# Scaling attention probabilities on ScalarE instead of VectorE and GpSimd

## The chip, the cores and the metric

One core of a Trainium2 chip runs the whole program. The metric is the device time of one execution in microseconds (us). The engines are TensorE (PE in the profile), VectorE (DVE), ScalarE (ACT), GpSimd (POOL) and SyncE (SP), which issues the DMAs. Each engine works through its own queue in order and waits for others by semaphores.

## The reference

Two layers of a hybrid backbone over 256 latent tokens and 256 context tokens of width 1024. Each layer has four parallel token mixers (differential attention, Hyena long convolution, a Conformer convolution, multi-head latent attention), a gated merge, an output projection, and a mixture of 16 experts. Layer 1 computes the latent tokens' outputs only. The change concerns two of the mixers:

```python
def attn_probs(q, k, scale):
    s = jnp.einsum('...qd,...kd->...qk', q, k).astype(jnp.float32) * scale
    return jax.nn.softmax(s, axis=-1)

def softmax_attend(q, k, v, scale):              # latent attention, 4 heads
    p = attn_probs(q, k, scale)
    return jnp.einsum('bhqk,bhkv->bhqv', p.astype(v.dtype), v)

def diff_attend(q, k, v, lam):                   # differential attention, 4 heads, two maps each
    p = attn_probs(q, k, DIFF_HEAD_DIM ** -0.5)
    a = p[:, :, 0] - lam * p[:, :, 1]
    return jnp.einsum('bhqk,bhkv->bhqv', a.astype(v.dtype), v)
```

Context queries see the 256 context keys only; latent queries see all 512 keys.

## The kernel before

Everything is float32; the large projections split each operand into a high and a low half and use three matmuls per product (`mm3`, L355 to L357). The halves are made by `split` (L346): ScalarE casts the high half (L348), VectorE subtracts for the low one (L349).

The program is written as generators, one for each thread of work: the input projection (`head`, `body`), `hyena`, `mla` (latent attention), `rope`, `diff` (differential attention), the four branch projections, the conformer, the modulation products (`products`, whose VectorE work is L510), and the experts with their router. A planner (`Order.run`, L175) keeps an estimated clock for each of PE, ACT, DVE and POOL. A generator emits some instructions and yields their estimated costs, as a dictionary by engine; the planner adds them to its clocks one after the other and picks as next the first generator in its list whose time has come. The order in which instructions are emitted is the order in each engine's queue, so the yielded costs fix the order of the whole program. The cost functions are `_a` for ScalarE, `_d` for VectorE and `_q` for GpSimd.

Attention is cut into units of 128 query rows and one head: 16 units in layer 0 (8 with 256 keys, 8 with 512), 8 in layer 1 (512 keys). Both loops are software pipelines over the units. In iteration i they scale the probabilities of unit i-1, transpose those of unit i-2 on TensorE (`transposed`, L1267: four transposes by matmul, then a ScalarE copy out of PSUM, L1272), multiply those of unit i-3 with the values, and compute scores and exponentials of unit i (`probs`, L1257: VectorE takes the row maximum, L1260, and negates it, L1262; ScalarE takes the exponential with a row sum, L1264).

In `mla` the scaling is a reciprocal of the row sum on VectorE (L1390) and a multiply of the probabilities by it (L1391). The multiply runs on VectorE in layer 0 and on GpSimd in layer 1, by the constant `MS = (0, 1)`.

In `diff` a unit has two maps, e0 and e1, and a pair of row sums. VectorE takes the reciprocals (L1493), multiplies e1 by its reciprocal and by minus lambda (L1494; `lamt` holds minus lambda), and adds e0 times its reciprocal to that (L1495). When the four heads of a query block are done, a head norm follows (L1531 to L1537), and its transposed outputs are split by L1509 on ScalarE and L1510 on VectorE.

Of the kernel before, what the change touches and what calls it, by code (L numbers as in the profile page):

```python
# [13 lines left out]
AF = mybir.ActivationFunctionType  # L14
OP = mybir.AluOpType
# [198 lines left out]
def _a(n):  # L214
    return 0.19 + n / 1200


def _d(n):
    return 0.07 + n / 960


def _q(n):
    return 0.1 + n / 480
# [3 lines left out]
def kernel(ctx: ExitStack, tc: tile.TileContext, x, ctxt, cols, skip, lamb, fng, ta, tb, tcn, td,  # L227
                       fwt, cc, ada_w, ada_t, w_in, w_uq, w_ukv, w_branch, w_out, w_ei, w_eo, out):
    nc = tc.nc
# [9 lines left out]
    LAG = (2.0, 1.0)  # L239
    PIECE = (4, 2)  # L240
    ORD = (0, 2)
    BA, MS, MVP = (1, 1), (0, 1), (1, 5)
    RINGS = ((1, 4), (2, 4))
    TGS, LOOK = (4, 10), 20.0
    GATE, F1, EXTRA, EARLY, EXTRA2 = 40, 9, (8, 8), (2, 3), (3, 4)
# [77 lines left out]
    lamt = const.tile([128, DEPTH], F32, name="lamt")  # L323
# [73 lines left out]
    def layer(l):  # L397
# [908 lines left out]
        def mla():  # L1306
# [17 lines left out]
            e = yield {"pe": 0.5, "dve": _d(512)}  # L1324
# [12 lines left out]
            e = yield rope_m(krT[R3, 256:])  # L1337
            km = [t2("km") for _ in range(4)]
            for hd in range(4):
# [4 lines left out]
                e = yield {"pe": 0.86, "act": _a(512), "pool": 0.8}  # L1344
# [40 lines left out]
            for i in range(n + 3):  # L1385
                end = []
                if 0 <= i - 1 < n:
                    nk = units[i - 1][2]
                    e, r = es.pop(i - 1)
                    nc.vector.reciprocal(r, r)  # L1390
                    (nc.gpsimd if MS[l] else nc.vector).tensor_scalar(e, e, r, None, op0=OP.mult)  # L1391
                    ws[i - 1], e = e, None
                    end.append((yield {"dve": 0.1, "pool" if MS[l] else "dve ": _q(nk) if MS[l] else _d(nk)}))
                if 0 <= i - 2 < n:
                    eTs[i - 2], cost = transposed(ws.pop(i - 2), units[i - 2][2])
                    end.append((yield cost))
                if 0 <= i - 3 < n and units[i - 3][3] % 2:
                    s, qc, nk, hd = units[i - 3]
                    oc, c = slice(qc - q0, qc - q0 + 128), hd // 2
                    if hd == 1:  # L1400
                        po = px()
                    pv = po[:, c * 128:(c + 1) * 128]
                    for k in range(nk // 128):
                        for j in range(2):
                            vo = (k % 2) * 256 + (2 * c + j) * 64
                            nc.tensor.matmul(pv[j * 64:(j + 1) * 64, :], mvt[k // 2][:, vo:vo + 64],
                                             eTs[i - 4 + j][:, k * 128:(k + 1) * 128],
                                             start=k == 0, stop=k == nk // 128 - 1, tile_position=(0, j * 64))
                    eTs.clear() if i - 2 >= n else [eTs.pop(u) for u in (i - 4, i - 3)]
                    hi, lo = o_ml[c]  # L1410
                    nc.scalar.copy(hi[:, oc], pv)
                    nc.vector.tensor_tensor(lo[:, oc], pv, hi[:, oc].bitcast(F32), op=OP.subtract)
                    end.append((yield {"pe": nk / 128 * 0.22, "act": _a(128), "dve": _d(128)}))
                if i < n:
                    s, qc, nk, hd = units[i]
                    p, r = psc(), sm(1, "re")
                    nc.tensor.matmul(p[:, :nk], qm[hd][:96, qc - q0:qc - q0 + 128], km[hd][:96, :nk], start=True, stop=True)
                    e, cost = probs(p, nk, scale, r)
                    es[i], p, e = (e, r), None, None
                    end.append((yield {"pe": nk * 0.00168, **cost}))  # L1420
                yield max(end) + LAG[l]
# [56 lines left out]
        def diff():  # L1478
            yield rope_ev["k"]
            yield rope_ev["q"]  # L1480
            rope_tab.clear()
            scale = 64.0 ** -0.5
            for c in range(4):
                o_df[c] = two("o")
            units = [(s, qc, nk, hd) for s, qc, nk in qblocks() for hd in range(4)]
            n = len(units)
            es, ws, eTs, os = {}, {}, {}, None
            for i in range(n + 4):
                end = []
                if 0 <= i - 1 < n:  # L1490
                    nk = units[i - 1][2]
                    e0, e1, r = es.pop(i - 1)
                    nc.vector.reciprocal(r, r)  # L1493
                    nc.vector.tensor_scalar(e1, e1, r[:, 1:2], lamt[:, l:l + 1], op0=OP.mult, op1=OP.mult)  # L1494
                    nc.vector.scalar_tensor_tensor(e0, e0, r[:, 0:1], e1, op0=OP.mult, op1=OP.add)  # L1495
                    ws[i - 1], e0, e1 = e0, None, None
                    end.append((yield {"dve": 0.1 + _d(nk) * 1.6}))
                if 0 <= i - 2 < n:
                    eTs[i - 2], cost = transposed(ws.pop(i - 2), units[i - 2][2])
                    end.append((yield cost))  # L1500
                if os is not None:
                    oc = slice(units[i - 4][1] - q0, units[i - 4][1] - q0 + 128)
                    p = pt()
                    for hh in range(4):
                        nc.tensor.transpose(p[:, hh * 128:(hh + 1) * 128], os[:, hh * 128:(hh + 1) * 128], ident)
                    for hh in range(4):
                        pv = p[:, hh * 128:(hh + 1) * 128]
                        hi, lo = o_df[hh]
                        nc.scalar.activation(hi[:, oc], pv, AF.Copy, scale=gsub)  # L1509
                        nc.vector.scalar_tensor_tensor(lo[:, oc], pv, gsub, hi[:, oc].bitcast(F32),  # L1510
                                                       op0=OP.mult, op1=OP.subtract)
                    os = None
                    end.append((yield {"pe": 0.5, "act": 4 * _a(128), "dve": 4 * _d(128)}))
                if i == 3:
                    for b in range(2):
                        yield dv_ev[b][0]
                    yield ml_done
                if 0 <= i - 3 < n:
                    s, qc, nk, hd = units[i - 3]
                    aT = eTs.pop(i - 3)  # L1520
                    if hd == 0:
                        po = px()
                    for k in range(nk // 128):
                        nc.tensor.matmul(po[:, hd * 128:(hd + 1) * 128], aT[:, k * 128:(k + 1) * 128],
                                         vd[k][:, hd * 128:(hd + 1) * 128], start=k == 0, stop=k == nk // 128 - 1)
                    aT = None
                    end.append((yield {"pe": nk / 128 * 0.21}))
                    if hd == 3:
                        os = t2("do")
                        ov = os.rearrange("p (h c) -> p h c", h=4)  # L1530
                        nc.scalar.activation(os, po, AF.Square)  # L1531
                        ss = sm(4, "ssd")
                        nc.vector.tensor_reduce(ss, ov, axis=AX.X, op=OP.add)
                        r = sm(4, "rsd")
                        rsqrt(r, ss, 1.0 / 128)
                        nc.vector.tensor_tensor(ov, po.rearrange("p (h c) -> p h c", h=4),
                                                r[:, :, None].to_broadcast([128, 4, 128]), op=OP.mult)  # L1537
                        end.append((yield {"act": _a(512), "dve": _d(512) + 0.1, "pool": 0.3, "dve ": _d(512)}))
                        if i - 3 == n - 1:
                            df_mid.t = S.t["pe"]  # L1540
                if i < n:
                    s, qc, nk, hd = units[i]
                    oc = slice(qc - q0, qc - q0 + 128)
                    pp, r = [psc(), psc()], sm(2, "re")
                    for c in range(2):
                        hs_ = slice(64 * c, 64 * c + 64)
                        nc.tensor.matmul(pp[c][:, :nk], qd[hd][hs_, oc], kd[hd][hs_, :nk], start=True, stop=True,
                                         tile_position=(64 * c, 0))
                    e0, cost = probs(pp[0], nk, scale, r[:, 0:1])
                    yield {"pe": nk * 0.00344, **cost}  # L1550
                    e1, cost = probs(pp[1], nk, scale, r[:, 1:2])
                    es[i], pp, e0, e1 = (e0, e1, r), None, None, None
                    end.append((yield cost))
                yield max(end) + LAG[l]
            end = max(end)
            drop(len(vbig))
            df_done.t = end
# [573 lines left out]
```

## Time and profile before

| | us |
|---|---|
| median of 3 runs | 2000.3 (1995.54 to 2003.92) |
| the profiled execution | 2003.71 |
| its span, first to last instruction | 2001.9 |
| TensorE busy | 1700.4 (85%) |
| VectorE busy | 971.6 (49%) |
| ScalarE busy | 461.8 (23%) |
| GpSimd busy | 217.3 (11%) |
| mean granted clock of TensorE | 0.913 |

Busy time is an average over stages of different kinds, so it is to be read stretch by stretch: the page has a row of 40 equal slices for each engine, about 50 us each. A chain of waits follows the last instruction back, at each step to what released it.

### The profile page before, as it was taken

How to read it: one execution, taken by the hardware profiler on the slowest of the kernel's cores; microseconds unless marked ns; L12 is line 12 of the kernel's file. 1: busy time of each engine (PE TensorE's matmuls, PEld its weight loads, DVE VectorE, ACT ScalarE, POOL GpSimd, SP SyncE). 2: the span in 40 equal slices, each digit the busy share in tenths (PEclk: the TensorE clock that was granted, in tenths of full speed). 3: DMA queues.
4: the chain of work that ended last, by engine and by line, in shares of the span. 5: the costliest groups of instructions: out<-in, count | busy, mean ns of one | idle time of the engine just before them, and what ended most of it. 6: DMA issues, size and time to landing. Idle time of an engine off the chain costs nothing.

```text
span 2001.9 us, 27922 instructions
## 1 busy us (share of the span) xinstructions
PE 1700.4 (85%) x11128; PEld 1108.5 (55%) x11128; DVE 971.6 (49%) x2052; ACT 461.8 (23%) x933; POOL 217.3 (11%) x229
## 2 busy tenths in 40 slices
PE   5998999887999899899899788998988867666665
PEld 2677788665679634333333278888987423322222
DVE  4886789877764312212432285888864111111012
ACT  4423333323332100100110063344442000000000
POOL 1322011021201000000010042410211000000000
PEclk8999999888999899989999998999998877787777
DMA  7443334423345799999999954565759999999997
GB/s 280 168 140 112 127 116 134 147 90 95 99 134 225 250 365 411 418 418 416 415 415 416 401 177 146 165 200 163 227 185 357 414 414 414 413 413 412 414 413 284
DMA packets 204586, 550.72 MB, mean 275 GB/s; under 512 B 14054, under 2 KB 94120, under 8 KB 173992
## 3 DMA queue, kind: packets, MB, share of 16 engines
q1 hardware_dynamic: 204456, 548.94, 72.8%
q8 instruction: 88, 1.44, 0.3%
q14 instruction: 42, 0.34, 0.1%
HBM read 547.83 MB, written 1.05 MB: 274 GB/s over the span
## 4 chain that ended last, share of the span: by engine, by line
PE 48%; DMA 26%; DVE 14%; issue 6%; ACT 5%; POOL 1%; SPq 0%; ACTq 0%; DVEq 0%; POOLq 0%
DMA we<-in_w_ei_dram 14%; PE pm L1951 10%; DMA we<-in_w_eo_dram 7%; PE pm L355 7%; PE pm L357 6%; PE pm L356 6%; PE psc L1976 4%; DVE wq L349 3%; DMA h<-in_w_eo_dram 3%; PE psc L1840 2%; DVE aw L510 2%; PE psc L355 2%; ACT wq L348 1%; PE psc L357 1%; PE psc L356 1%
## 5 line engine op out<-in xcount | busy, mean ns | idle before, releaser
L1951 PE MATMUL pm<-we,xe 128*32 128x256 f32 (+1 forms) x2912 | 406.9, 542 | 96.3 <-DMA we<-in_w_ei_dram 94.4
L1951 PEld LDWEIGHTS pm<-we,xe 128*32 128x32 f32 (+1 forms) x2912 | 136.7, 136 | 343.3 <-issue 185.2
L355 PE MATMUL pm<-uh,wq 128*128 128x256 f32 (+1 forms) x832 | 293.4, 353 | 7.4 <-ACT wq L348 4.8
L356 PE MATMUL pm<-ul,wq 128*128 128x256 f32 (+1 forms) x832 | 283.7, 341 | 2.4 <-DVE ul L754 1.5
L357 PE MATMUL pm<-uh,wq 128*128 128x256 f32 (+1 forms) x832 | 283.2, 340 | 0.0
L1963 DVE SCALAR_TENSOR_TENSOR ea<-ea,pm 128x512 f32<-128x512 f32 (+1 forms) x32 | 17.7, 554 | 426.7 <-ACT ea L1962 426.7
L349 DVE TENSOR_TENSOR wq<-wi,wq 128x1024 fp32r<-128x1024 f32 x131 | 164.1, 1263 | 91.9 <-ACT wq L348 91.5
L1976 PE MATMUL psc<-we,eaT 128*32 128x256 f32 (+1 forms) x1280 | 170.9, 506 | 39.8 <-DMA we<-in_w_eo_dram 37.8
L355 PEld LDWEIGHTS pm<-uh,wq 128*128 128x128 f32 x832 | 161.9, 195 | 29.8 <-ACT wq L348 6.5
L356 PEld LDWEIGHTS pm<-ul,wq 128*128 128x128 f32 x832 | 162.2, 195 | 20.6 <-issue 3.9
L357 PEld LDWEIGHTS pm<-uh,wq 128*128 128x128 f32 x832 | 161.8, 194 | 16.8
L1988 DVE TENSOR_TENSOR ye<-psc,modr 32x512 f32<-32x512 f32 (+1 forms) x120 | 66.4, 553 | 204.8 <-PE psc L1976 203.4
L1976 PEld LDWEIGHTS psc<-we,eaT 128*32 128x32 f32 (+1 forms) x1280 | 58.3, 128 | 146.8 <-issue 74.8
L348 ACT CAST wq<-wi 128x1024 fp32r<-128x1024 f32 x132 | 136.1, 1043 | 10.7 <-DMA wi<-in_w_in_dram 9.3
L1962 ACT ACTIVATE ea<-pm 128x512 f32<-128x512 f32 (+1 forms) x32 | 15.7, 491 | 481.0 <-PE pm L1951 481.0
L1218 DVE SCALAR_TENSOR_TENSOR ca<-up,colt,ca 128x510 f32<-128x510 f32 (+29 forms) x120 | 80.8, 673 | 2.1
L355 PE MATMUL pm<-wq,uh 128*128 128x256 f32 (+1 forms) x240 | 72.7, 303 | 8.1 <-DVE rsq L319 4.0
L2020 ACT COPY eaT<-pt 128x512 f32<-128x512 f32 (+1 forms) x32 | 15.3, 479 | 278.2 <-PE pt L2018 278.2
L510 DVE SCALAR_TENSOR_TENSOR aw<-aw,h 128x512 f32<-128x512 f32 x96 | 77.1, 803 | 3.6
L1264 ACT ACTIVATE e<-psc,nm 128x512 f32<-128x512 f32 (+1 forms) x72 | 44.5, 618 | 146.8 <-DVE nm L1262 144.4
L356 PE MATMUL pm<-wq,uh 128*128 128x256 f32 (+1 forms) x240 | 70.7, 295 | 0.0
L357 PE MATMUL pm<-wq,ul 128*128 128x256 f32 (+1 forms) x240 | 70.7, 295 | 0.0
(407 smaller groups left out, 2639.0 us busy)
## 6 DMA issues: line engine op xcount, KB each, us to landing
we<-in_w_ei_dram SPq DMA_DIRECT2D x233, 1024.0 KB, 13.0
we<-in_w_eo_dram SPq DMA_DIRECT2D x110, 1024.0 KB, 14.6
wi<-in_w_in_dram SPq DMA_DIRECT2D x58, 1024.0 KB, 5.4
aw<-in_ada_t_dram SPq DMA_DIRECT2D x160, 256.0 KB, 5.3
we<-in_w_ei_dram SPq DMA_DIRECT2D x52, 256.0 KB, 9.0
wbr<-in_w_branch_dram SPq DMA_DIRECT2D x40, 256.0 KB, 5.6
h<-in_w_ei_dram SPq DMA_DIRECT2D x40, 256.0 KB, 16.2
h<-in_w_eo_dram SPq DMA_DIRECT2D x40, 256.0 KB, 16.2
```

Source lines behind the costliest of these rows:

```text
L348: nc.scalar.copy(hi, src)
L349: eng.tensor_tensor(lo, src, hi.bitcast(F32), op=OP.subtract)
L355: nc.tensor.matmul(out, lh, rh, start=first and i == 0, stop=False)
L356: nc.tensor.matmul(out, lh, rl, start=False, stop=False)
L357: nc.tensor.matmul(out, ll, rh, start=False, stop=last and i == n - 1)
L510: nc.vector.scalar_tensor_tensor(o, wt_, 1.0, cb[s, k], op0=OP.mult, op1=OP.mult, accum_out=ends[lm, g][0][:, s, c, k:k + 1])
L1218: nc.vector.scalar_tensor_tensor(o, up[:, :, max(d, 0):256 + min(d, 0)], cw[:, c0 + d:c0 + d + 1], o, op0=OP.mult, op1=OP.add)
L1264: nc.scalar.activation(e, p[:, :nk], AF.Exp, scale=scale, bias=nm, accum_out=s)
L1840: nc.tensor.matmul(p[:, kk * n:(kk + 1) * n], h[2 * s + b][k // 4][:, (k % 4) * 128:(k % 4 + 1) * 128], hot[:, 2 * i + b], start=b == 0, s ...
L1951: nc.tensor.matmul(dst[j * M:(j + 1) * M, :], lhs, w[o + j * FW // 512][:, j * FW % 512:j * FW % 512 + FW], start=k == 0, stop=k == KC - 1 ...
L1976: nc.tensor.matmul(py[j * M:(j + 1) * M, :FW], aT[:, c * 128 + q * M:c * 128 + (q + 1) * M], w[f % 2 * 2 + j * FW // 512][:, j * FW % 512: ...
L1988: nc.vector.tensor_tensor(ye[eg][s][c0 // 512][e4 * CAP:(e4 + 1) * CAP, c0 % 512:c0 % 512 + FW], py[r0:r0 + CAP, :FW], mod5[r0:r0 + CAP, c ...
```

## The change

In latent attention both layers now multiply the probabilities on ScalarE, by a copy with a scale per row; the constant `MS` goes. In differential attention the reciprocal of the second map's row sum is first multiplied by minus lambda, one number per row, on VectorE; ScalarE then scales the second map by that factor, and VectorE adds the first map as before. The costs that the two generators yield to the planner change with it.

```diff
-    BA, MS, MVP = (1, 1), (0, 1), (1, 5)
+    BA, MVP = (1, 1), (1, 5)
...
                     nc.vector.reciprocal(r, r)
-                    (nc.gpsimd if MS[l] else nc.vector).tensor_scalar(e, e, r, None, op0=OP.mult)
+                    nc.scalar.activation(e, e, AF.Copy, scale=r)
                     ws[i - 1], e = e, None
-                    end.append((yield {"dve": 0.1, "pool" if MS[l] else "dve ": _q(nk) if MS[l] else _d(nk)}))
+                    end.append((yield {"dve": 0.1, "act": _a(nk)}))
...
                     nc.vector.reciprocal(r, r)
-                    nc.vector.tensor_scalar(e1, e1, r[:, 1:2], lamt[:, l:l + 1], op0=OP.mult, op1=OP.mult)
+                    nc.vector.tensor_tensor(r[:, 1:2], r[:, 1:2], lamt[:, l:l + 1], op=OP.mult)
+                    nc.scalar.activation(e1, e1, AF.Copy, scale=r[:, 1:2])
                     nc.vector.scalar_tensor_tensor(e0, e0, r[:, 0:1], e1, op0=OP.mult, op1=OP.add)
                     ws[i - 1], e0, e1 = e0, None, None
-                    end.append((yield {"dve": 0.1 + _d(nk) * 1.6}))
+                    end.append((yield {"dve": 0.2, "act": _a(nk), "dve ": _d(nk)}))
```

## Rows read from the trace of the kernel before

**Rows 1.** The page's slices: busy tenths, 40 slices of 50 us each.

```profile
PE   5998999887999899899899788998988867666665
...
DVE  4886789877764312212432285888864111111012
...
DMA  7443334423345799999999954565759999999997
```

**Rows 2.** Busy time by stretch: length, busy us and instructions per engine, clock, DMA.

```profile
225.00:360.00 135.00, 134.34 (x745) 110.13 (x744) 118.06 (x275) 49.93 (x107) 15.50 (x16) 1.00 0.42 135
390.00:490.00 100.00, 76.66 (x344) 58.37 (x343) 73.83 (x173) 33.80 (x73) 21.27 (x23) 0.88 0.29 90
490.00:560.00 70.00, 65.20 (x307) 51.19 (x307) 53.81 (x113) 22.44 (x43) 14.18 (x11) 0.95 0.33 105
1262.00:1320.00 58.00, 57.71 (x439) 50.77 (x438) 51.74 (x121) 24.01 (x49) 29.25 (x24) 1.00 0.59 186
1372.00:1405.00 33.00, 27.00 (x195) 25.71 (x194) 23.74 (x52) 14.79 (x29) 2.11 (x2) 0.90 0.50 162
```

**Rows 3.** Chain of waits, stretches of differential attention: start us, us, what.

```profile
397.06 0.42 DVE e L1494
397.51 0.48 DVE e L1495
...
479.67 0.38 ACT oh L1509
480.07 0.36 DVE ol L1510
...
545.47 0.56 DVE e L1494
546.05 0.75 DVE e L1495
...
1383.83 0.56 DVE e L1494
```

**Rows 4.** Waits from 370 to 540 us: us in total, times, longest.

```profile
ACT e L1264 <- DVE nm L1262: 53.4, 18, 6.6
...
PE psc L355 <- ACT wbrh L348: 19.4, 2, 12.4
```

**Rows 5.** Groups by line and shape: busy us, mean ns, idle time before.

```profile
L1391 POOL TENSOR_SCALAR e<-e,re 128x512 f32<-128x512 f32 x8 | 13.0, 1625 | 14.3 <-DVE re L1390 7.0 <-issue 4.6 <-PE px L1406 2.8
...
L1391 DVE TENSOR_SCALAR e<-e,re 128x512 f32<-128x512 f32 x8 | 4.8, 594 | 0.3
...
L1391 DVE TENSOR_SCALAR e<-e,re 128x256 f32<-128x256 f32 x8 | 3.4, 424 | 0.3
```

**Rows 6.** Groups by line and shape on ScalarE.

```profile
L374 ACT ACTIVATE acc<-acc,rs 128x512 f32<-128x512 f32 x4 | 2.8, 712 | 0.4 <-POOL rs L370 0.4
...
L1361 ACT ACTIVATE cqT<-pt,colt 128x256 f32<-128x256 f32 x2 | 0.8, 478 | 0.0
...
L348 ACT CAST wq<-wi 128x1024 fp32r<-128x1024 f32 x132 | 136.1, 1043 | 10.7 <-DMA wi<-in_w_in_dram 9.3 <-issue 1.4
```

**Rows 7.** Order in time, layer 1, GpSimd and VectorE: start us, us, instruction.

```profile
1283.35 1.57 POOL L1391 TENSOR_SCALAR e<-e,re 128x512 f32<-128x512 f32 x1 [1.34 <-DVE re L1390]
...
1283.99 0.68 DVE L510 SCALAR_TENSOR_TENSOR aw<-aw,cb 128x512 f32<-128x512 f32 x1
...
1310.24 1.57 POOL L1391 TENSOR_SCALAR e<-e,re 128x512 f32<-128x512 f32 x1
...
1310.34 1.36 DVE L1218 SCALAR_TENSOR_TENSOR ca<-up,colt,ca 128x243 f32<-128x243 f32 x2
```

**Rows 8.** Order in time, VectorE, one differential unit.

```profile
450.80 0.16 DVE L1493 RECIPROCAL re<-re 128x2 f32<-128x2 f32 x1
451.00 0.55 DVE L1494 TENSOR_SCALAR e<-e,re,lamt 128x512 f32<-128x512 f32 x1
```

**Rows 9.** Order in time, ScalarE, behind the unit of 461 us.

```profile
461.58 0.62 ACT L1062 CAST oh<-cx 128x512 fp32r<-128x512 f32 x1 [2.92 <-DVE cx L1250]
```

## The prediction

> **What bounds the kernel now.** I read the page's slices first, then the busy time by stretch, then the chain of waits, then the rows of the instructions that the change touches. The slices [rows 1] show two kinds of stage. In slices 12 to 22 and 30 to 39 the DMA engines are 90% busy or more: these are the expert layers, which wait for weights, and the change has nothing in them. In between lie the mixers, where TensorE and VectorE are both at 70 to 99%. The change lies only there: latent attention and differential attention of layer 0 (225 to 560 us) and of layer 1 (1262 to 1405 us).
>
> These stretches differ [rows 2]. From 225 to 360 us TensorE is busy 134.3 of 135 us at full clock, and from 1262 to 1320 us 57.7 of 58: both latent attentions lie there, and TensorE bounds them. From 390 to 490 us TensorE is busy 76.7 of 100 us and VectorE 73.8: nothing is full, and the granted clock is 0.88. There the chain of waits runs for long through VectorE with hops to ScalarE, and the units of differential attention are on it [rows 3]. One such hop is the wait of 12.4 us in which TensorE has nothing to do until ScalarE casts a branch weight [rows 4]; ScalarE in turn had waited for VectorE's row maximum (53.4 us over 18 times between 370 and 540 us). So the price of the change is read from the chain between 390 and 560 us, not from the busy shares.
>
> **The change part by part.** The profiled execution took 2003.7 us (span 2001.9); the median of the runs is 2000.3, 3.4 less. Differences are worked out on the profiled one and added to the median.
>
> *Latent attention, layer 0, 16 units.* VectorE loses eight multiplies of 0.42 us (256 wide) and eight of 0.59 us (512 wide) [rows 5]: 3.4 + 4.8 = 8.1 us. ScalarE gains as many copies with a per-row scale. The nearest rows are 0.71 us for 512 columns from SBUF and 0.48 us for 256 (read from PSUM) [rows 6]: 3.8 + 5.7 = 9.5 us. Path: nothing either way. TensorE is idle for 0.7 us in those 135 us [rows 2], so no VectorE time given back can be seen there, and ScalarE, busy 49.9 of 135 us, has the room. Behind the reciprocal VectorE still does a row maximum and its negation before ScalarE can take the next exponential, so the copy fits into time in which ScalarE waits for VectorE anyway. If that cover were gone the cost would be at most the 9.5 us. The gain is bounded by the 8.1 us, if VectorE came so much earlier into the stretch after 390 us.
>
> *Latent attention, layer 1, 8 units.* GpSimd loses eight multiplies of 1.63 us, 13.0 us [rows 5]; ScalarE gains eight copies of 0.71, 5.7 us. Path: nothing. TensorE is full (57.7 of 58 us), and ScalarE is busy 24.0 of 58. What GpSimd does next, the rotation of the keys and queries, starts earlier, but TensorE, full as it is, would not show it.
>
> There is a contention that could go. GpSimd's multiply at 1310.24 us lies beside a pair of convolution taps on VectorE that takes 1.36 us; the one at 1283.35 us lies beside a product that takes 0.68 us, what such products take with no GpSimd work beside them [rows 7]. So VectorE loses a few tenths of a us in some of the eight, about 1 us in all by my estimate (0.4 us in two or three of eight).
>
> The Trainium skill ("SBUF — State Buffer", section "Who interferes with whom") says that a VectorE instruction with two SBUF inputs and a GpSimd instruction that reads SBUF exclude each other for the whole instruction of the one that came first. The pair of taps agrees with it; the product at 1283.99, which has two such inputs and runs 0.68 us inside the GpSimd multiply, does not show it. By that rule VectorE would get up to 13.0 us back in layer 1 and not 1, and the sum below would still be the same, since TensorE is full there; it raises the chance of the third rival a little.
>
> *Differential attention, 24 units (16 in layer 0, 8 in layer 1).* Before, VectorE does reciprocal, multiply by row factor and minus lambda, and the fused multiply-add, one after the other with no other engine. After, it does the reciprocal, a multiply of one column, then waits for ScalarE's copy, then the multiply-add. The start of the multiply-add comes after the start of the first multiply by 0.45 us at 256 columns and 0.58 us at 512 [rows 3]. In its place stand: the one-column multiply, 0.20 us as from the reciprocal to its successor [rows 8]; the handover to ScalarE; the copy, 0.48 or 0.71 us; the handover back. ScalarE's copy at 479.67 us ends at 480.05 and VectorE goes on at 480.07 [rows 3], so two handovers are about 0.10 us. Sums: 0.78 against 0.45 is +0.33 us for 256 columns, 1.01 against 0.58 is +0.43 us for 512. That holds if ScalarE stands idle when the factor is ready. The bounds: 0 if the wait falls into time in which VectorE would have waited for something else; one weight cast of 1.04 us more [rows 6] if ScalarE has just begun one.
>
> Queued behind the waiting multiply-add on VectorE are the row maxima of the next unit, the low halves of weight casts, and the modulation products; ScalarE's exponential, then its casts, then TensorE wait for those. On ScalarE, the copy waits for the reciprocal, and what stands behind it waits too.
>
> On the chain of waits the multiply of such a unit appears nine times in layer 0, four of 256 columns (the first at 397.06 us) and five of 512 (the last at 545.47), and once in layer 1 (1383.83) [rows 3]. The other 14 run beside TensorE's matmuls or beside another link of the chain; I take them at 0. Sum: 4 x 0.33 + 6 x 0.43 = 3.9 us. At one of the units, after 461 us, ScalarE is at a cast of 0.62 us when VectorE gets there [rows 9], and its square for the head norm, which VectorE needs next, then stands behind the copy: about +0.7. Together **+4.6 us**.
>
> *The order.* The kernel's planner lays out all instructions by the costs that the generators yield, and these change (GpSimd or VectorE to ScalarE in one loop; a longer VectorE stay in the other). So other instructions change places as well. No row prices that. One such accident of order is worth up to the 12.4 us wait [rows 4], in either direction. I take 0 for it and keep plus or minus 12 for the range.
>
> **The forecast**: 2000.3 + 4.6 = **2005 us**, +0.23%, within what a measurement of this kernel can tell from no change (about 0.5%, 10 us).
>
> **The rivals.**
> 1. *ScalarE's queue becomes the block (slower).* ScalarE now stops at every differential unit until VectorE has come to its reciprocal, where before it ran ahead with weight casts, and the casts behind feed VectorE and TensorE. If each of the ten units on the chain holds up one cast of 1.04 us more, that is +10.4 on top of 4.6: 2015 us. It decides where TensorE has no matmuls left to cover, from 390 to 490 us, where the clock of 0.88 shows what idle time does to it. For it: VectorE and ScalarE already wait for each other there. Against: at 11 of the 12 units I looked up ScalarE was idle when the reciprocal came.
> 2. *All of it is hidden.* The +0.4 us each fall into waits that are there anyway: 2000 us. For it: ScalarE is busy a third of the stretch only. Against: the ten multiplies are on the chain.
> 3. *VectorE's relief counts (faster).* The planner hands the 8.1 us freed in layer 0 to modulation products that now crowd the stretch after 390 us, and the new order undoes the 12.4 us wait: 2000.3 - 8.1 - 12.4 + 4.6 = 1984 us. For it: VectorE is at 118 of 135 us before 360 us, so the products are what fills it. Against: it needs both; with one of them alone the time is 1992 to 1997, no change by measure.
>
> **How the numbers follow.** Forecast 0.45 (own range 2001 to 2010), rival 1 0.25, rival 2 0.15, rival 3 0.15. Slower by over 0.5% is above 2010.3: most of rival 1 and an edge of the forecast, 0.23. Faster by over 0.5% is below 1990.3: most of rival 3, 0.13. The rest, 0.64, is no change. The range takes in rival 1 with a little more and stops short of rival 3's full price: 1988 to 2017.
>
> **What would show it.** In the changed profile: no multiply of that line on GpSimd or VectorE in latent attention, 24 more ScalarE copies there of 0.5 and 0.7 us, TensorE still full between 225 and 360 and between 1262 and 1320 us. In differential attention a VectorE wait before each multiply-add, released by ScalarE's copy, some 0.6 to 0.8 us each, 14 to 19 us in all, and the stretch between 360 and 560 us longer by about 4 us. I am wrong on the wait if its mean is over 1.2 us (rival 1) or if the chain no longer passes these units (rival 2), and wrong on the order if a TensorE wait of over 5 us comes or goes at a place that has no attention unit in it.

## The result, and the profile after

The changed kernel takes 2020.5 us (median of four runs, 2013.5 to 2026.1) against 1999.7 us: 1.0090 of before, interval [1.0070, 1.0111], slower by some 18 us (14 to 22). The two medians differ by 20.8 us; the ratio of the runs, which has the interval, is used from here on. The forecast was +4.6 us and a range that ended at 2017. The profiled execution has a span of 2017.5 us.

VectorE is busy 952.6 us (before 971.6), ScalarE 488.4 (461.8), GpSimd 205.7 (217.3), TensorE 1697.5 (1700.4). No engine but ScalarE has more to do, and the time is lost all the same. The page's slices, as in [rows 1]:

```profile
PE   5998999888979899899899788998978766776565
...
DVE  4886777776774312212432285876864111111012
...
DMA  7443333422346799999999944544867999999997
```

The busy time by stretch, columns as in [rows 2]: length, busy us and instructions of TensorE, its weight loads, VectorE, ScalarE and GpSimd, clock, DMA.

```profile
225.00:360.00 135.00, 132.61 (x729) 108.86 (x729) 101.56 (x233) 55.54 (x120) 15.55 (x16) 0.99 0.39 123
390.00:490.00 100.00, 83.36 (x373) 64.06 (x373) 72.58 (x169) 37.62 (x80) 23.43 (x24) 0.93 0.28 88
490.00:560.00 70.00, 65.52 (x313) 51.01 (x311) 48.26 (x109) 28.94 (x56) 10.66 (x8) 0.98 0.31 98
1264.00:1322.00 58.00, 58.00 (x431) 50.65 (x431) 46.31 (x107) 28.26 (x55) 15.93 (x16) 1.00 0.51 164
...
1505.00:1548.00 43.00, 32.98 (x252) 32.49 (x252) 17.34 (x40) 10.67 (x27) 5.52 (x8) 0.83 0.59 205
```

TensorE is still nearly full in the two latent attentions, as forecast (idle 2.4 us in the first, 0.7 before, and not at all in the second). The stretch 390 to 490 us is even fuller than before, since the planner's new order moved work into it. Layer 0 as a whole loses little: its first router matmul starts at 640.6 us, 3.2 later. Layer 1's output projection ends 18.8 us later than before. The last row shows where much of that is: 10 of 43 us without a matmul, at a mean granted clock of 0.83.

The touched instructions, by line and shape (against [rows 5, 6]): busy us, mean ns, idle time of the engine before them and what ended it. L1391 is now a ScalarE copy, L1495 the other one, L1494 the one-column multiply, L1496 the multiply-add.

```profile
L1496 DVE SCALAR_TENSOR_TENSOR e<-e,re 128x512 f32<-128x512 f32 x16 | 12.3, 766 | 13.6 <-ACT e L1495 13.6
L1391 ACT ACTIVATE e<-e,re 128x512 f32<-128x512 f32 x16 | 11.6, 723 | 25.7 <-DVE re L1390 25.7
L1495 ACT ACTIVATE e<-e,re 128x512 f32<-128x512 f32 x16 | 11.6, 723 | 43.7 <-DVE re L1494 43.7
L1494 DVE TENSOR_TENSOR re<-re,lamt 128x1 f32<-128x1 f32 x24 | 6.0, 250 | 0.8
L1391 ACT ACTIVATE e<-e,re 128x256 f32<-128x256 f32 x8 | 4.1, 511 | 26.2 <-DVE re L1390 26.2
```

The copies take 723 and 511 ns, near the forecast's 0.71 and 0.48. VectorE's waits over the whole run (us in total, times, longest) show the wait that was expected, 0.80 us in the mean. They also show one that was not: the low half of the latent output, L1412, waits for its cast, 18.8 us in all, of which the kernel before has 0.5:

```profile
DVE e L1496 <- ACT e L1495: 19.1, 24, 1.0
...
DVE ohl L1412 <- ACT ohl L1411: 9.7, 4, 4.7
DVE ol L1412 <- ACT oh L1411: 9.1, 7, 1.5
```

One unit on VectorE in order of time, as in [rows 8]; in brackets the idle time before it. From reciprocal to multiply-add it is 1.20 us, against 0.78 before:

```profile
455.34 0.16 DVE L1493 RECIPROCAL re<-re 128x2 f32<-128x2 f32 x1
455.53 0.16 DVE L1494 TENSOR_TENSOR re<-re,lamt 128x1 f32<-128x1 f32 x1
456.54 0.75 DVE L1496 SCALAR_TENSOR_TENSOR e<-e,re 128x512 f32<-128x512 f32 x1 [0.85 <-ACT e L1495]
```

TensorE's waits: between 370 and 540 us the branch weight of [rows 4] costs 11.1 us instead of 19.4. Between 1420 and 1550 us the same wait, 1.4 us before, is now

```profile
PE psc L355 <- ACT wbrh L348: 12.9, 2, 10.7
```

The chain of waits says why. Nine expert loads were issued just ahead, the last four of them here; then one branch weight is under way for 11.69 us, ScalarE casts it, and only then does TensorE go on:

```profile
1498.76 0.50 SPq L1677
1499.31 0.43 SPq L1677
1499.79 0.45 SPq L1677
1500.34 0.41 SPq L1677
1500.85 11.69 DMA wbr<-in_w_branch_dram
1512.56 0.63 ACT wbrh L348
1513.23 0.58 PE psc L355
```

So there were two theories: the new instructions cost, by waits in queues that run in order; or the new order of everything else costs, by a load that comes late.

### The profile page after: what moved, and what is told of

Its sections match the earlier page's. It is cut to its first block, busy times and chain, and to the rows that moved or that the text cites. A ratio compares the mean times of both kernels' runs of the same rounds, so it can differ in the third digit from the quotient of the medians.

```text
span 2017.5 us, 27963 instructions
## 1 busy us (share of the span) xinstructions
PE 1697.5 (84%) x11128; PEld 1107.9 (55%) x11128; DVE 952.6 (47%) x2036; ACT 488.4 (24%) x981; POOL 205.7 (10%) x221
## 4 chain that ended last, share of the span: by engine, by line
PE 51%; DMA 24%; DVE 11%; issue 7%; ACT 5%; POOL 1%; SPq 0%; ACTq 0%; DVEq 0%; POOLq 0%
PE pm L1952 12%; DMA we<-in_w_ei_dram 11%; DMA we<-in_w_eo_dram 9%; PE pm L355 7%; PE pm L357 6%; PE pm L356 6%; PE psc L1977 5%; DVE wq L349 2%; PE psc L1841 2%; PE psc L355 2%; PE psc L357 2%; PE psc L356 1%; DVE aw L510 1%; ACT wq L348 1%; DMA aw<-in_ada_w_dram 1%
## 5 line engine op out<-in xcount | busy, mean ns | idle before, releaser
L1952 PE MATMUL pm<-we,xe 128*32 128x256 f32 (+1 forms) x2832 | 397.1, 543 | 96.4 <-DMA we<-in_w_ei_dram 94.6
L1977 PE MATMUL psc<-we,eaT 128*32 128x256 f32 (+1 forms) x1360 | 177.2, 503 | 42.9 <-DMA we<-in_w_eo_dram 41.2
## 6 DMA issues: line engine op xcount, KB each, us to landing
h<-in_w_ei_dram SPq DMA_DIRECT2D x60, 256.0 KB, 13.2
```

Of the source, the lines that this page charges most:

```text
L1952: nc.tensor.matmul(dst[j * M:(j + 1) * M, :], lhs, w[o + j * FW // 512][:, j * FW % 512:j * FW % 512 + FW], start=k == 0, stop=k == KC - 1 ...
L1977: nc.tensor.matmul(py[j * M:(j + 1) * M, :FW], aT[:, c * 128 + q * M:c * 128 + (q + 1) * M], w[f % 2 * 2 + j * FW // 512][:, j * FW % 512: ...
```

## The experiments

Ratios to the kernel before, with 95% intervals. "Old costs" means that the generators yield the costs of before, so that TensorE's and SyncE's queues are those of before, instruction by instruction.

| run | ratio | interval |
|---|---|---|
| changed kernel | 1.0090 | 1.0070 to 1.0111 |
| e1 new instructions, old costs | 1.0093 | 1.0075 to 1.0111 |
| e2 old instructions, new costs | 1.0037 | 1.0023 to 1.0052 |
| e3 latent loop only, its new costs | 1.0062 | 1.0045 to 1.0078 |
| e4 differential loop only, its new costs | 1.0121 | 1.0104 to 1.0138 |
| e5 latent copy, old costs | 0.9996 | 0.9985 to 1.0008 |
| e6 differential copy, old costs | 1.0057 | 1.0040 to 1.0074 |
| e7 latent copy placed later, old costs | 0.9990 | 0.9979 to 1.0000 |
| e8 changed kernel, branch weights two ahead | 1.0128 | 1.0111 to 1.0145 |
| e9 multiply-add placed later, old costs | 0.9990 | 0.9978 to 1.0002 |
| e10 differential copy twice, old costs | 1.0162 | 1.0143 to 1.0182 |
| e11 changed kernel, one load ahead of nine | 1.0057 | 1.0035 to 1.0079 |
| e12 both placed later, old costs | 0.9992 | 0.9976 to 1.0008 |
| e13 latent later, differential in place, old costs | 1.0039 | 1.0018 to 1.0060 |
| e14 old instructions, new order, load ahead | 0.9994 | 0.9984 to 1.0004 |
| e15 all the change, with the three repairs | 1.0003 | 0.9992 to 1.0014 |

### Instructions or order (e1 to e4)

e1 has the two loops' new instructions and old `yield` lines; e2 the reverse; e3 and e4 both lines of one loop.

```diff
 e1
-                    (nc.gpsimd if MS[l] else nc.vector).tensor_scalar(e, e, r, None, op0=OP.mult)
+                    nc.scalar.activation(e, e, AF.Copy, scale=r)
...
 e2
...
-                    end.append((yield {"dve": 0.1 + _d(nk) * 1.6}))
+                    end.append((yield {"dve": 0.2, "act": _a(nk), "dve ": _d(nk)}))
```

> The changed instructions in both loops, but the two generators yield the costs of before, so that TensorE's and SyncE's queues hold the same instructions in the same order as before. Theory A (the order that the planner makes from the new costs is the loss): 2000 to 2006 us, no more than the 4 us of added waits. Theory B (the copies in ScalarE's queue are the loss: what stands behind them, VectorE's waits for ScalarE above all, comes late whatever the order): 2013 to 2022 us.

> The instructions of before in both loops, but the generators yield the costs of the change, so TensorE's and SyncE's queues have the order of the changed kernel. Theory A (order): 2013 to 2022 us, with the wait of some 10 us for a branch weight's DMA near the end of layer 1's mixer as in the changed kernel. Theory B (ScalarE's queue): 1996 to 2005 us.

> Only latent attention changed (copies on ScalarE, with their new costs); differential attention as before. If the loss comes from latent attention in layer 1, where VectorE's low half of the output waits for ScalarE's cast behind copy and transposed copy (9.7 us in four waits, 0.5 us before): 2010 to 2020 us. If it comes from differential attention's added waits: 1996 to 2003 us. Theory A leaves either open, since any change of costs makes a new order.

> Only differential attention changed (minus lambda into the row factor, copy on ScalarE, new costs); latent attention as before. By the added waits of differential attention alone, as predicted: 2004 to 2006 us. If latent attention is the loss: 2000 to 2005. If the sum of both orders matters (theory A): anywhere from 1995 to 2020, not the difference of the full change and the latent-only kernel.

Both cost: the instructions 0.93% in the old order, the order 0.37% with the old instructions. They don't add up to 1.30% but to 0.90%: beside the new instructions the new order costs nothing net. Of the expectations, e1 came out as theory B had it; e2 (2010.9 us) lies between the ranges of its two theories, and e4 (2026.5) above all that was named for it. e3 (2016.0) lies in the range that was named for latent attention, but it has the late branch weight, and e5 below shows that the latent copy alone costs nothing. The runs with one loop (0.62 and 1.21%) each have an order of their own, and e2, e3 and e4 all have the late branch weight of layer 1, as the changed kernel has: 10.4, 10.9 and 12.3 us of TensorE's time in its longest wait, which neither before nor e1 shows (0.7).

### Which loop (e5, e6)

```diff
 e6
-                    nc.vector.tensor_scalar(e1, e1, r[:, 1:2], lamt[:, l:l + 1], op0=OP.mult, op1=OP.mult)
+                    nc.vector.tensor_tensor(r[:, 1:2], r[:, 1:2], lamt[:, l:l + 1], op=OP.mult); nc.scalar.activation(e1, e1, AF.Copy, scale=r[:, 1:2])
```

e5 is the latent line of e1 alone.

> Latent attention scales on ScalarE in both layers, differential attention as before, the old yielded costs, so TensorE's and SyncE's queues are those of the kernel before. The same instructions in both loops cost +17.5 us in the run with the old costs (2020.3 against 2002.8). Theory A (the copy stands ahead of the transposed copy and of the cast of the latent output in ScalarE's queue, so ScalarE, VectorE and TensorE go in step): at least half of it comes back here, +8 to +12 us, and the waits of the low half (L1412) for the cast (L1411) are again 12 us or more against 0.5 before. Rival B (only the wait in differential attention costs): within +-3 us of before, whatever those waits are.

> Differential attention scales its second map on ScalarE, latent attention as before, the old yielded costs and so the old order of TensorE's and SyncE's queues. Theory A (the latent loop costs half or more): +5 to +9 us. Rival B (the wait in differential attention is all of it): +15 to +18 us. The forecast on record, 10 units on the chain at 0.33 and 0.43 us, would give +4 to +5. The wait of the multiply-add for the copy should be 0.6 to 1.0 us in each of 24 units, 15 to 23 us in all.

Theory A of these texts fell: the latent copy in front of its unit's casts makes the waits that it named (two rows, e5) and costs nothing.

```profile
DVE ol L1412 <- ACT oh L1411: 7.8, 7, 1.5
DVE ohl L1412 <- ACT ohl L1411: 4.4, 3, 1.5
```

The differential copy alone costs 0.57%, 11.4 us (8.0 to 14.8), which lies between the ranges of theory A and rival B. Its wait, in e6:

```profile
DVE e L1495 <- ACT e L1494: 22.6, 24, 2.4
```

The same unit in e6 as in [rows 8], VectorE in order of time:

```profile
454.94 0.16 DVE L1493 RECIPROCAL re<-re 128x2 f32<-128x2 f32 x1
455.14 0.16 DVE L1494 TENSOR_TENSOR re<-re,lamt 128x1 f32<-128x1 f32 x1
456.15 0.75 DVE L1495 SCALAR_TENSOR_TENSOR e<-e,re 128x512 f32<-128x512 f32 x1 [0.85 <-ACT e L1494]
456.82 0.69 DVE L1260 TENSOR_REDUCE mx<-psc 128x1 f32<-128x512 f32 x1
```

From L1494 to the multiply-add it is 1.01 us, against 0.58 before: +0.43, as the forecast had it. Read in this way for all 24 units (start of the reciprocal to start of the multiply-add, e6 less before), 15 lie at 0.34 to 0.35 (256 columns) or 0.42 to 0.44 (512); the sum is 13.6 us. All 24 at 0.33 and 0.43 would be 9.5; the other 4.1 are a few longer ones, above all two in layer 1 with 1.61 and 2.02. For the latter, ScalarE in order of time shows the cause: in its queue a copy of a TensorE result stands ahead, which waits 2.95 us for TensorE.

```profile
1350.92 0.37 ACT L1451 COPY vd<-pm 128x256 f32<-128x256 f32 x1 [2.95 <-PE pm L357]
1351.19 0.72 ACT L1494 ACTIVATE e<-e,re 128x512 f32<-128x512 f32 x1
```

How much of this was paid shows on TensorE, whose queue in e6 is that of before, so that stretches between the same matmuls can be compared (columns as in [rows 2]; before, then e6, for layer 0 and for layer 1; one profiled execution each, that of e6 the slowest of its four):

```profile
360.00:600.00 240.00, 200.84 (x912) 156.38 (x911) 179.12 (x392) 79.69 (x159) 39.08 (x38) 0.91 0.35 110
362.50:611.20 248.70, 204.19 (x912) 158.36 (x911) 176.65 (x393) 86.87 (x172) 38.82 (x38) 0.88 0.33 107
1320.00:1400.00 80.00, 73.30 (x551) 66.18 (x550) 64.77 (x142) 37.91 (x77) 1.04 (x1) 0.96 0.55 169
1332.00:1416.50 84.50, 74.89 (x551) 67.13 (x549) 61.23 (x142) 42.28 (x84) 1.04 (x1) 0.94 0.52 160
```

The stretch of layer 0 is 8.7 us longer and holds thirteen units whose additions sum to 5.7 us; that of layer 1 is 4.5 us longer, with eight units and 6.2 us. The first three units lie beside the matmuls of latent attention, and there TensorE fell back by 0.7 us (225 to 360 us) for additions of 1.7. So about the sum of the additions was paid, but not unit by unit. Of the 13.2 us of the two stretches 8.3 are idle time of TensorE; in the other 4.9 it is busy longer with the same matmuls, at a mean granted clock of 0.88 instead of 0.91 and 0.94 instead of 0.96.

### Is the wait the price (e9, e10)

```diff
 e9 (on e6): ahead of "yield max(end) + LAG[l]", at the end of the iteration
-                    nc.vector.scalar_tensor_tensor(e0, e0, r[:, 0:1], e1, op0=OP.mult, op1=OP.add)
...
-                yield max(end) + LAG[l]
+                late and (nc.vector.scalar_tensor_tensor(late[0], late[0], late[2][:, 0:1], late[1], op0=OP.mult, op1=OP.add), ws.__setitem__(i - 1, late[0])); late = None; yield max(end) + LAG[l]
 e10 (on e6): behind the copy, in its line
+                    ...; nc.scalar.activation(e1, e1, AF.Copy, scale=1.0)
```

> As the run with the differential copy alone and the old costs (2014.8 against 2001.4 us; 24 waits of VectorE for the copy, 22.6 us), but each unit's multiply-add stands on VectorE behind the row maxima of the next unit; TensorE's, ScalarE's, GpSimd's and SyncE's queues are the same. Theory A (VectorE standing in that wait is the price, all 24 units of it): the wait falls under 4 us in all and the time to 1999 to 2004 us, or below by up to the 8 us that VectorE no longer has to do. Rival B (ScalarE's longer queue, or the copy's place in it, is the price): it stays at 2012 us or more though the wait is gone. Rival C (the weights come later because the multiply-add does, and the transposes wait instead): TensorE's transposes (L1270) wait for L1554, and the time is between.

> As the run with the differential copy alone and the old costs, but ScalarE copies the second map a second time, by 1.0, ahead of the multiply-add: the wait grows by one copy, 0.51 or 0.72 us, 15.6 us over 24 units. Theory A (every unit's wait is paid in full): +15 us on the 2014.8 us, 2027 to 2033 us. The forecast's count (10 of 24 units on the chain): +6, 2019 to 2022 us. Rival (some slack was used up by the first copy, and the second is paid more than in full, since ScalarE then holds up casts too): 2035 us or more.

VectorE's wait in e9, where the multiply-add is L1554, then in e10:

```profile
DVE e L1554 <- ACT e L1494: 1.1, 2, 0.9
```

```profile
DVE e L1495 <- ACT e L1494: 38.4, 24, 4.6
```

Without the wait the price is gone (0.9990), with ScalarE's work and all other queues unchanged; TensorE's transposes wait 2.2 us in all for the later multiply-add. With the second copy the additions sum to 29.4 us, and the time is longer by 32.4 us (28.6 to 36.4). Both are as theory A had it. So a us of standing in this wait costs about a us, at all units together. The stretch from 360 to 600 us of before, 240.0 us at a mean granted clock of 0.91, takes 236.6 at 0.92 in e9 and 255.3 at 0.89 in e10. VectorE's relief in e9, 14.0 us of multiplies less 6.1 of one-column ones and 1.1 of waiting, 6.8 us, moves the time by -2.0 us (-4.4 to +0.4): almost none of it comes back.

### The latent copy's place (e7, e13, e12)

```diff
 e7 (on e5): the copy behind the transposed copy and the cast, ahead of the next scores
-                    nc.scalar.activation(e, e, AF.Copy, scale=r)
...
+                late and (nc.scalar.activation(late[0], late[0], AF.Copy, scale=late[1]), ws.__setitem__(i - 1, late[0]))
```

e13 is e6 and e7 together; e12 is e9 and e7.

> As the run with latent attention alone and the old costs, but each unit's copy stands on ScalarE behind the transposed copy and the cast of the same iteration, ahead of the next exponential; VectorE's, TensorE's and SyncE's queues stay. Theory A: the waits of L1412 for L1411 fall to below 3 us in all, and the loss of the run with the copy in front falls to +3 us or less. Rival B: the time is that of the run with the copy in front (the place of the copy in the queue does not matter). Rival C (any copy more on ScalarE in this loop costs by its length): the same too.

> Both loops scale on ScalarE with the old costs; the latent copy stands behind the transposed copy and the cast, the differential multiply-add in its first place. All queues but ScalarE's are those of the run with both copies in front (2020.3 us, ratio 1.0093); with the differential copy alone the ratio was 1.0057, with the latent copy alone 0.9996. Theory (the 7 us by which the two together cost more than their sum are the latent copy's place in ScalarE's queue, which counts only where VectorE has no slack left): ratio 1.005 to 1.007. Rival (the 7 us come from the two copies' work on ScalarE, wherever they stand): 1.008 to 1.011.

> Both loops scale on ScalarE with the old costs, the latent copy behind the transposed copy and the cast, the differential multiply-add behind the row maxima of the next unit. With both in front and the old costs it was 2020.3 us (+17.5). Theory A (places in the in-order queues are the whole price of the instructions): 1995 to 2003 us, no slower than before. Rival (ScalarE's 26 us more work in these stretches costs by itself): 2008 us or more.

In e7 the waits of L1412 are back at 1.0 us in all, and the time is that of e5: alone, the place is worth nothing. Beside the differential waits it is worth 0.54% (e1 1.0093, e13 1.0039), so the copy's work on ScalarE is not the price; e13 came out even below the range of its theory, and its runs spread widely (2002.3 to 2016.1 us). How the place comes to cost is not shown. It is not by the waits of L1412 themselves: in e1 they are 12.2 us as in e5, all before 360 us or between 1307 and 1333 us, and over the stretches of before that hold them (225 to 360, 1262 to 1320 us) TensorE, with the same queue, falls back only 1.5 us more in e1 than in e13. It falls back 3.4 us more between 360 and 600 us and 2.2 more between 1320 and 1400. That VectorE has no slack left there is a reading of this, not a result. In e12 both places are mended and the price is gone (0.9992), as its theory had it.

### The order (e8, e11, e14, e15)

```diff
 e8 (on the changed kernel)
-    BA, MVP = (1, 1), (1, 5)
+    BA, MVP = (1, 2), (1, 5)
 e11 (on the changed kernel), e14 (on e2), in layer 1: hold is set from branch 2's third load to its fourth,
 and what is held is issued behind the fourth
+        hold, held = [False], []; we_dma = lambda dst, src: held.append((dst, src)) if hold[0] else nc.sync.dma_start(dst, src)
...
-                            nc.sync.dma_start(w[q], src)
+                            we_dma(w[q], src)
...
```

> The changed kernel, but in layer 1 the branch weights are loaded two column blocks ahead and not one. Theory (the new order costs because the last branch weight's load lands late, TensorE waiting 10.7 us at 1500 to 1525 us): the wait falls under 1 us and the time to 2010 to 2013 us, against 2020.5 for the changed kernel. Rival (the expert layer of layer 1 is bound by its weight loads, which this only puts back; the time between is then given back later): 2017 to 2022 us with the wait gone. A second rival: the earlier loads need other buffers and change the order once more, in which case the time can go either way by 5 us or more with no TensorE wait for a branch weight left.

> The changed kernel with one edit to SyncE's queue: in layer 1 the last load of the branch weights of the conformer's branch is issued ahead of the nine loads of expert weights that stood before it. All other queues are the same, instruction by instruction. Theory (the 10.7 us in which TensorE waits for that weight in layer 1 are what the new order costs there): the wait falls under 2 us and the time by 7 to 10 us, to 2010 to 2014 us. Rival (the expert layer behind it is bound by its loads, which are put back by that one, or the wait only changes its releaser): 2018 us or more.

> The old instructions in the order of the changed kernel (2010.9 us, ratio 1.0037), with the one branch weight load of layer 1 issued ahead of nine expert loads, as in the run that did so to the changed kernel (which fell by 8.7 us). Theory (that load is the whole price of the new order): ratio 0.998 to 1.001. Rival (the new order has other prices, and the load only hides them): 1.002 or more, the time given back elsewhere.

> All of the change with its new costs, with the three repairs: latent copy behind the transposed copy and cast, differential multiply-add behind the next row maxima, the branch weight load ahead of the nine expert loads. Theory (the change's loss is these three places and nothing else): 0.996 to 1.001 of before, 17 us or more below the changed kernel; a gain of more than 0.3% over before only if VectorE's relief (19 us in the changed kernel's busy time) is on the path anywhere. Rival (the three repairs do not add up): 1.003 or more.

e8 says little: its change of a parameter made yet another order, and its time (2029.1 us) lies outside the ranges of its theory and of the first rival. The wait for the weight is short (3.2 us at the longest), but TensorE now waits longer for the exponentials (14.4 us in all, 7.3 in the changed kernel), and the time is 0.4% longer than that of the changed kernel. TensorE's waits, 1300 to 1550 us:

```profile
PE psc L355 <- ACT e L1264: 14.4, 4, 5.0
PE psc L355 <- ACT wbrh L348: 7.2, 4, 3.2
```

e11 changes one place in SyncE's queue and nothing else. TensorE's wait for the weight, 1420 to 1550 us:

```profile
PE psc L355 <- ACT wbrh L348: 4.3, 2, 2.2
```

It gives back 8.7 us by the medians (2020.5 to 2011.8 us, on different chips) and 6.6 by the ratios (1.0090 to 1.0057), whose intervals overlap; the wait was to fall under 2 us and is 2.2 at the longest. In e14 the same place takes the whole price of the order away (1.0037 to 0.9994, intervals apart). e15 has all of the change with the three places mended and is level with the kernel before: with these three mended nothing of the loss is left. None of the versions is faster than before by more than its interval; the best two, e7 and e9, stand at 0.9990.

## Why the prediction was wrong

- **What bounds.** Right: TensorE stays nearly full in the latent attentions, and nothing is gained there.
- **Latent attention at nothing.** Right where it was taken alone (e5, 0.9996), wrong as a term of this sum: in the old order its place cost 0.54% beside the other edit (e1 against e13). The step looked at how much time ScalarE had (49.9 of 135 us) and not at what stands behind the copy in ScalarE's queue: the copy waits for the reciprocal, and the transposed copy and the cast wait with it. By which wait this is paid stays open.
- **The differential unit, +0.33 and +0.43 us.** Right to 0.02 us at most units; the wait's mean in the changed kernel is 0.80 us, within the 0.6 to 0.8 that was named.
- **"The other 14 run beside TensorE's matmuls or beside another link of the chain; I take them at 0."** This step failed. Alone the edit cost 11.4 us (e6) against 3.9; all 24 units at the forecast's own prices would be 9.5, and a few longer waits add about 4. It shows best in layer 1, where the chain has one unit, 0.43 us, and e6 lost 4.5. The chain names one path of several that are nearly as long; which units were paid singly is not shown, and about a third of the loss on TensorE is not idle time but the same matmuls taking longer at a lower granted clock.
- **The order at 0, plus or minus 12.** A term that was mis-sized: with the old instructions the order cost 7.4 us (e2), inside the 12. The row that was read for it, the 12.4 us of [rows 4], showed the size and even the kind: a branch weight that comes late, now at another place, for 10.7 us. The price of this load is 0.33% (e11) to 0.43% (e2 against e14). The text's own mark for this failure, a TensorE wait of over 5 us that comes at a place without an attention unit, is what the trace shows. Beside the new instructions, though, the order cost nothing net (1.0090 against 1.0093 of e1): it also gave time back in layer 0, where the wait of [rows 4] is 11.1 us instead of 17.2 in e1, and the first router matmul starts at 640.6 us instead of 645.0. So the miss is the instructions: 18.6 us (15.0 to 22.2) in the old order against 4.6.
- **The sum.** 11.4 (the differential wait) and 6.6 to 8.6 (the load) are 18 to 20 us; measured 18 (14 to 22). That they agree is in part luck: the first is a price in the old order, where both copies together cost 18.6 us with no late load, and the second one in the new. What the latent copy's place costs in the changed order is not measured by itself; with the load ahead, e11 stands at the 1.0057 that the differential copy costs alone in the old order.
- **The rivals.** Rival 1 had the direction and nearly the time (2015 us), but not the mechanism: the wait's mean is 0.80 us, and in the longest wait of e6 ScalarE is held by a copy of a TensorE result that stands ahead, not by a weight cast. Its remark on the clock is borne out: from 360 to 600 us the mean granted clock is 0.88 in e6, 0.91 before. Rival 3's relief of VectorE came, 19.0 us of busy time, and is worth nothing that can be measured (e9, e12, e15).
- **Readings.** The chain of the kernel before also passes a unit of 256 columns at 339.35 us, so it has eleven, and the sum of 3.9 us would be 4.2. The DMA digits of [rows 1] are 9 in slices 14 to 22 and 30 to 38, counted from 0, and VectorE's digits beside them run from 3 to 9. The pair of taps at 1310.34 us does not agree with a lock for the whole instruction: its first tap takes 0.85 us, 0.38 more than the second, and both end by 1311.70, before GpSimd's multiply does at 1311.81. The estimate of about 1 us was near: the eighteen taps that start between 1262 and 1320 us take 10.9 us before and 9.9 in e5. None of this changes the forecast by more than 0.3 us.

## What to carry to other kernels

Before moving an operation to an idle engine, read what stands behind it in that engine's queue and what then stands behind the hop back; here the hops in the middle of a unit cost about as much as they added over all 24 units, though the chain shown passes fewer than half of them. The hop was free where the waiting instruction was put behind work that is ready: one place each in two loops turned +0.9% into nothing (e1, e12). When a planner's costs are edited, test the new order with the old instructions, and look at where the loads fall in the DMA queue.

## What was not expected of the hardware

A copy with a per-row scale takes 723 ns at 512 columns, the same copy with a constant scale 631 ns; both stand in e10's groups:

```profile
L1494 ACT ACTIVATE e<-e,re 128x512 f32<-128x512 f32 x16 | 11.6, 723 | 37.4 <-DVE re L1494 37.4
L1494 ACT ACTIVATE e<-e 128x512 f32<-128x512 f32 x16 | 10.1, 631 | 0.5
```

The 92 ns agree with the Trainium skill ("ScalarE: Activation LUTs", section "What ACT_TABLE_LOAD costs"), which has about 93 ns for each per-row operand.

A load of 256 KB that was issued behind nine expert loads (five of 1 MB, four of 256 KB) landed after 11.69 us; the median of these loads between 1455 and 1520 us is 4.5 us.
